# Down product of a SwiGLU layer: three stretches of eight contraction tiles by a seven-product scheme

## Chip, cores and metric

The kernel runs on one core of a Trainium2 chip. The metric is the device time of one execution in microseconds (us), median of several runs. Beside it stands one execution that was taken with the hardware profiler. Its engines are PE (matmul; PEld is its weight load), DVE (vector), ACT (scalar), POOL (GpSimd) and SP (which only issues DMAs here; a "q" behind an engine's name, as in SPq, is its queue).

## What is computed

One decoder layer on 544 tokens (512 of a prompt and 32 of samples), model width 2048. Its last part is the one that matters here:

```python
def layer_tail(x, attn_out, pool_out, w_out, norm_ffn, w_gate, w_up, w_down):
    x = x + jnp.concatenate([attn_out, pool_out], axis=-1) @ w_out
    h = rmsnorm(x, norm_ffn)
    return x + (jax.nn.silu(h @ w_gate) * (h @ w_up)) @ w_down
...
    y_prompt = rmsnorm(xp, norm_final)
    y_sample = rmsnorm(xs, norm_final)
```

All arrays are fp32. `w_gate` and `w_up` are 2048 x 5632, `w_down` is 5632 x 2048.

## The kernel before

Activations are kept transposed: features on 128 partitions, the 544 tokens along the free dimension. Width 2048 is 16 feature tiles, and the inner width 5632 is 44 tiles. Every factor of a product is split into a high and a low part (`whi`/`wlo` for weights, `H`/`L` for activations), and a product is three matmuls: high by high, high by low, low by high. The high part is a copy by ACT into a rounded type, the low part a subtraction on DVE. One matmul takes a 128 x 128 weight tile and 272 token columns, half of the 544.

**The gate and up products** (class `Winograd`, L874 to L993) use a scheme with seven block products in place of eight. Weights and activations are each cut into 2 x 2 blocks (output tiles p and p + 22 by the two halves of the contraction; the halves of the contraction by the two halves of the tokens). For each of 44 pairs of output tiles seven products P1 to P7 run on PE, each on sums or differences of blocks. Products are gathered in three PSUM tiles: X takes P1, then P6, P7 and P4 on top of it; Y takes P2; Z takes P5, then P3. After each step the partial sum is read before the next product is added to the same tile. The order within a pair is P2, P6, P5, P7, then P1 of the next pair, P4, P3. Sums of weight blocks are partly made by DMA: SP loads one block (`a11`, `a12`, `s1`, `s3`, `a22`), and POOL issues a second DMA that adds another block to `s1` and `s3`. DVE makes two more sums (`s2` at L949, `s4` at L961). `prep` and `high` (L920 to L965) run ACT and DVE up to four weight units ahead of PE.

In `ff_out` (L1003) ACT reads X after P1, P6 and P7 (`cp`, L1010), and DVE adds the pieces (L1013 to L1020). The results go to DRAM (`gd`).

**The down product** (L1233 to L1258) is plain. The 44 contraction tiles are taken in chunks of 12, 12, 12, 4 and 4. For each of the first four chunks, and for each of 16 output tiles `nt`, PE runs 6 matmuls for each contraction tile (`mm3`, L193: two halves of the tokens, three matmuls each). DVE then adds the PSUM tile to `x2` in SBUF, 544 columns at a time (L1252). Weights come through class `Stream` (L115): SP loads units of four contraction tiles into four `raw` buffers, ACT makes the high part (L143), DVE the low part (L148), some three units ahead of PE. The activations of the next chunk are loaded from `gd` by the generator `load_g` (L1155) one step for each `nt`; its first run starts in the last eight products of the gate and up part, with two steps for each product (L1195). The last four contraction tiles run in a loop of their own (L1268 to L1298) with 272 columns at a time, interleaved with the final norm and the output.

What sets the order: there is no scheduler. Each engine runs its instructions in the order in which the program was written, and waits at an instruction until what it needs is there. SP and POOL issue DMAs in order too, and each issue waits for a free buffer.

```python
            for u in range(n // UW):
                ...
                wh, wl, _ = ws2.next()
                gH, gL = groups[u]
                for i in range(UW):
                    k = UW * u + i
                    mm3(acc, wh, wl, gH, gL, i, i, k == 0, k == n - 1)
            ...
            nc.vector.tensor_add(two(x2[:, nt]), acc[:, :, :HALF], two(x2[:, nt]))
```

Of the kernel before, what the change touches and what calls it, by code (L numbers as in the profile page):

```python
# [18 lines left out]
P = 128  # L19
# [27 lines left out]
CHUNK = 12  # L47


F_ORDER = list(range(12)) + list(range(22, 34)) + list(range(12, 21)) + list(range(34, 37)) + [21] + list(range(37, 44))  # L50
# [113 lines left out]
def program(ctx, tc, a):  # L164
# [79 lines left out]
    UW = 4  # L244
# [15 lines left out]
    chunks = [(0, CHUNK), (CHUNK, CHUNK), (2 * CHUNK, CHUNK), (3 * CHUNK, UW), (3 * CHUNK + UW, UW)]  # L260
# [613 lines left out]
    class Winograd:  # L874


        P1, P2, P6, P5, P7, P4, P3 = range(7)
        ORDER = (P2, P6, P5, P7, P1, P4, P3)

        def __init__(self, pairs, raw, ops, sums, out):  # L880
            self.pairs, self.raw, self.ops, self.sums, self.out = pairs, raw, ops, sums, out

            seq = [(0, self.P1), (0, self.P2), (1, self.P1), (1, self.P2)]
            for i in range(len(pairs)):
                for p in self.ORDER:
                    seq.append((i + 1, p) if p == self.P1 else (i, p))
            self.seq = [x for n, x in enumerate(seq) if x[0] < len(pairs) and x not in seq[:n]]
            self.np = self.nh = self.nl = 0
            self.q, self.s, self.parts, self.bank, self.cp = {}, {}, {}, {}, {}
            self.later = deque()  # L890

        def load(self, upto):
            while self.nl < min(upto, len(self.pairs)):
                i = self.nl
                for what in ("a11", "a12", "s1", "s3", "a22"):
                    for u in range(2):
                        self.load_unit(i, what, u)
                self.nl += 1

        def load_unit(self, i, what, u):  # L900
            if (i, what, u) in self.q:
                return

            pool, tag, bufs = self.raw[{(0, "a12"): "a11", (1, "a11"): "a12"}.get((i, what), what)]
            t = pool.tile([P, UW, P], F32, name=what, tag=tag, bufs=bufs)
            w, n0, n1 = self.pairs[i]

            def part(r, c):
                k = (HK if c == 2 else 0) + UW * u
# [5 lines left out]
            if i:  # L915
                for x in terms[1:]:
                    nc.gpsimd.dma_start(t, part(*x), accum_op=ALU.add)
            self.q[i, what, u] = t

        def prep(self, upto):  # L920
            upto = min(upto, 2 * len(self.seq))
            while self.np < upto:
                while self.nh < min(2 * len(self.seq), self.np + 2) and self.ready(self.nh):
                    self.high()
                x, hi = self.parts[self.np]
                lo = wpa.tile([P, UW, P], F32R, tag="wlo", name="wlo", bufs=4)
                nc.vector.tensor_sub(lo, x, hi.bitcast(F32))  # L927
                self.parts[self.np] = (hi, lo)
                self.np += 1

        def ready(self, n):
            (i, p), u = self.seq[n // 2], n % 2
            needs = {self.P1: "a11", self.P2: "a12", self.P6: "a22"}
            return p not in needs or (i, needs[p], u) in self.q

        def high(self):
            if True:
                (i, p), u = self.seq[self.nh // 2], self.nh % 2
# [6 lines left out]
                elif p == self.P6:  # L945
                    x = self.s[i, u] = new("s2")
                    if i == 0:
                        nc.vector.tensor_add(r("s1"), r("s1"), r("a22"))
                    nc.vector.tensor_add(x, r("s1"), r("a11"))  # L949
                    if i == 0:  # L950
# [16 lines left out]
        def run(self, between=None):  # L967
            for n, (i, p) in enumerate(self.seq):
                if p == self.P1 and i != 1:
                    self.load(i + 2)  # L970
                if (i, p) == (0, self.P4):
# [6 lines left out]
                bh, bl = self.ops(p)  # L978
                for u in range(2):
                    self.prep(2 * n + u + 3)  # L980
                    ahead = self.nh - 1
                    if self.later and self.seq[ahead // 2][1] not in (self.P6, self.P7, self.P3):
                        self.later.popleft()()
                    wh, wl = self.parts.pop(2 * n + u)
                    for j in range(UW):
                        k = UW * u + j
                        first, last = start and k == 0, k == HK - 1
                        nc.tensor.matmul(o, wh[:, j], bh[:, k], start=first, stop=False, skip_group_check=True)  # L988
                        nc.tensor.matmul(o, wh[:, j], bl[:, k], start=False, stop=False, skip_group_check=True)  # L989
                        nc.tensor.matmul(o, wl[:, j], bh[:, k], start=False, stop=last, skip_group_check=True)  # L990
# [4 lines left out]
    fc = ExitStack()  # L995
    pC = None
    gd = [dr.tile([P, 2, TOK], F32, name=f"gd{i}") for i in range(HF)]
    pairs = [(a[w], p, p + HF) for p in range(HF) for w in ("w_gate", "w_up")]
# [48 lines left out]
    wn = Winograd(pairs, raws, lambda p: ops[p], None, ff_out)  # L1047
# [66 lines left out]
    pC = fc.enter_context(tc.tile_pool(name="pC", bufs=1, space=PSUM))  # L1114
# [16 lines left out]
    def between(n):  # L1131
# [11 lines left out]
        if 3 <= n < 7:  # L1143
            for k in (2 * n - 6, 2 * n - 5):
# [6 lines left out]
    ws2 = Stream(nc, wpa, [a["w_down"][nt][:, k:k + UW, :] for c, n in chunks[:-1] for nt in range(KT)  # L1151
                           for k in range(c, c + n, UW)], UW, 4, 2, 2)
    parts = {}

    def load_g(ci):  # L1155

        c0, n = chunks[ci]
        groups, staged = [], deque()
        parts[ci] = groups
# [7 lines left out]
        for f in range(n):  # L1167
            if f % UW == 0:
                b = 3 * (ci % 2) + f // UW
# [17 lines left out]
    g0 = load_g(0)  # L1187
    N1 = len(wn.seq)

    def between1(n):  # L1190
# [3 lines left out]
        if n >= N1 - 8:  # L1194
            run(g0, 2)  # L1195
# [6 lines left out]
    pac2 = ctx.enter_context(tc.tile_pool(name="pac2", bufs=1, space=PSUM))  # L1202
    x2 = fq.tile([P, KT, TOK], F32, name="x2")
    ssum3 = fq.tile([P, TOK], F32, name="ssum3")
    flip = [0]
# [7 lines left out]

    lastw, lastr = {}, {}

    def last_load(nt):
        if nt < KT:
            lastr[nt] = wpa.tile([P, UW, P], F32, tag="raw", name="raw", bufs=4)
            dma(lastr[nt], a["w_down"][nt][:, chunks[-1][0]:, :])

    def last_high(nt):
        if nt < KT:
            if nt % 4 == 0:
                b = (1, 2, 4, 5)[nt // 4]
                lastw[nt // 4] = [bp.tile([P, 17, P], F32R, name=f"w{x}{b}", tag=f"b{x}{b}") for x in "HL"]
            nc.scalar.activation(lastw[nt // 4][0][:, nt % 4 * UW:(nt % 4 + 1) * UW], lastr[nt], AF.Copy)

    def last_low(nt):
        if nt < KT:
            h, l = (x[:, nt % 4 * UW:(nt % 4 + 1) * UW] for x in lastw[nt // 4])  # L1230
            nc.vector.tensor_sub(l, lastr.pop(nt), h.bitcast(F32))

    for ci, (c0, n) in enumerate(chunks[:-1]):  # L1233
        groups = parts.pop(ci)
        ahead = load_g(ci + 1)
        for nt in range(KT):
            if ci == 0:
                dma(x2[:, nt], x1d[nt])
            acc = acc4()
            for u in range(n // UW):  # L1240
                if ci == nt == 0:
                    run(g0, 10 ** 6 if u == n // UW - 1 else 2)
                wh, wl, _ = ws2.next()
                gH, gL = groups[u]
                for i in range(UW):
                    k = UW * u + i
                    mm3(acc, wh, wl, gH, gL, i, i, k == 0, k == n - 1)
            if nt > 0:
                run(ahead, 1)
            if ci == 0 and wn.later:  # L1250
                wn.later.popleft()()
            nc.vector.tensor_add(two(x2[:, nt]), acc[:, :, :HALF], two(x2[:, nt]))  # L1252
            if ci == len(chunks) - 2 and nt >= KT - 3:
                last_load(nt - KT + 3)
                if nt == KT - 1:
                    last_high(0)
                    last_high(1)
                    last_low(0)  # L1258

    (gH, gL), = parts.pop(len(chunks) - 1)  # L1260
# [7 lines left out]
    for h in range(2):  # L1268
        c = slice(h * HALF, (h + 1) * HALF)
        for nt in range(KT):  # L1270
# [17 lines left out]
            else:  # L1288
                sq = fq.tile([P, HALF], F32, name="sq3", tag="sq3", bufs=2)
# [66 lines left out]
```

## Time and profile before

| | |
|---|---|
| time, median of 3 runs | 2271.59 us (2268.67 to 2272.65) |
| time of the profiled execution | 2271.41 us |
| its span, first to last instruction | 2269.6 us |
| PE busy | 2236.1 us, 99% of the span |
| PE weight load busy | 2142.4 us, 94% |
| DVE busy | 1276.4 us, 56% |
| ACT busy | 853.5 us, 38% |
| POOL busy | 154.5 us, 7% |
| mean granted TensorE clock | 0.995 |

A busy share is the mean over the whole span. In time order the stages are: the input projections and the attention up to about 572 us, the output projection up to 774 us, gate and up from 774 to 1717 us, the down product from 1718 us, its last four contraction tiles from 2203 us, and the end of the final norm with the output. What a change in one stage is worth is read in that stage. Rows overlap: PE rows are pipelined, and successive DVE and ACT rows start before the one in front has ended, so a row's duration is longer than the step from one row to the next.

### The profile page before, as it was taken

How to read it: one execution, taken by the hardware profiler on the slowest of the kernel's cores; microseconds unless marked ns; L12 is line 12 of the kernel's file. 1: busy time of each engine (PE TensorE's matmuls, PEld its weight loads, DVE VectorE, ACT ScalarE, POOL GpSimd, SP SyncE). 2: the span in 40 equal slices, each digit the busy share in tenths (PEclk: the TensorE clock that was granted, in tenths of full speed). 3: DMA queues.
4: the chain of work that ended last, by engine and by line, in shares of the span. 5: the costliest groups of instructions: out<-in, count | busy, mean ns of one | idle time of the engine just before them, and what ended most of it. 6: DMA issues, size and time to landing. Idle time of an engine off the chain costs nothing.

```text
span 2269.6 us, 44020 instructions
## 1 busy us (share of the span) xinstructions
PE 2236.1 (99%) x17540; PEld 2142.4 (94%) x17540; DVE 1276.4 (56%) x2487; ACT 853.5 (38%) x1621; POOL 154.5 (7%) x200
## 2 busy tenths in 40 slices
PE   8999999999999999999999999999999999999997
PEld 8878787879999999999999999999999999999997
DVE  7644445476544576666666666666675333333356
ACT  6322222223333454444444444444453222222235
POOL 0000000000000011111111111111110000000000
PEclk9999999999999999999999999999999999999998
DMA  5665656576544577777777777777765533333233
GB/s 192 203 221 202 224 200 234 204 206 157 139 126 136 171 193 180 192 196 176 193 197 174 190 201 173 190 202 174 191 171 162 162 119 114 123 103 90 84 109 111
DMA packets 196138, 384.93 MB, mean 170 GB/s; under 512 B 32907, under 2 KB 38171, under 8 KB 192348
## 3 DMA queue, kind: packets, MB, share of 16 engines
q1 hardware_dynamic: 170784, 336.84, 46.9%
q0 software_dynamic: 24768, 45.10, 11.9%
q8 instruction: 137, 2.24, 0.4%
q14 instruction: 69, 0.57, 0.1%
q10 hardware_dynamic: 380, 0.18, 0.0%
HBM read 352.47 MB, written 29.56 MB: 168 GB/s over the span
## 4 chain that ended last, share of the span: by engine, by line
PE 96%; DVE 2%; DMA 1%; ACT 1%; issue 1%; SPq 0%; DVEq 0%; ACTq 0%
PE acc L197 16%; PE acc L199 15%; PE acc L198 15%; PE X L989 8%; PE X L988 8%; PE X L990 8%; PE Z L989 4%; PE Z L988 4%; PE Z L990 4%; PE Y L989 2%; PE Y L990 2%; PE Y L988 2%; PE SO L635 1%; PE SS L588 1%; PE S L519 1%; PE O L565 1%
## 5 line engine op out<-in xcount | busy, mean ns | idle before, releaser
L989 PE MATMUL X<-bL,whi 128*128 128x272 f32 x1408 | 409.8, 291 | 0.1
L988 PE MATMUL X<-bH,whi 128*128 128x272 f32 x1408 | 406.8, 289 | 1.7 <-ACT cp L1010 1.7
L990 PE MATMUL X<-bH,wlo 128*128 128x272 f32 x1408 | 406.7, 289 | 0.0
L143 ACT ACTIVATE whi<-raw 128x512 fp32r<-128x512 f32 x352 | 217.8, 627 | 479.3 <-PE acc L198 441.5
L197 PE MATMUL acc<-gH,whi 128*128 128x272 f32 x1280 | 371.0, 290 | 0.6 <-DVE gu L1020 0.6
L199 PE MATMUL acc<-gH,wlo 128*128 128x272 f32 x1280 | 370.5, 289 | 0.0
L198 PE MATMUL acc<-gL,whi 128*128 128x272 f32 x1280 | 368.5, 288 | 0.0
L197 PE MATMUL acc<-hH,whi 128*128 128x272 f32 x992 | 304.6, 307 | 5.4 <-ACT whi L143 5.4
L199 PE MATMUL acc<-hH,wlo 128*128 128x272 f32 x992 | 287.9, 290 | 0.8 <-DVE wlo L148 0.8
L198 PE MATMUL acc<-hL,whi 128*128 128x272 f32 x992 | 286.0, 288 | 0.0
L148 DVE TENSOR_TENSOR wlo<-raw,whi 128x512 fp32r<-128x512 f32 x352 | 236.0, 684 | 86.4 <-issue 78.0
L963 ACT ACTIVATE whi<-s 128x512 fp32r<-128x512 f32 x352 | 212.1, 627 | 184.4 <-DVE s L949 118.4
L927 DVE TENSOR_TENSOR wlo<-s,whi 128x512 fp32r<-128x512 f32 x352 | 237.7, 685 | 59.5 <-ACT whi L963 59.5
L988 PEld LDWEIGHTS X<-bH,whi 128*128 128x128 f32 x1408 | 266.5, 189 | 1.9 <-ACT cp L1010 1.9
L990 PEld LDWEIGHTS X<-bH,wlo 128*128 128x128 f32 x1408 | 266.0, 189 | 0.0
L989 PEld LDWEIGHTS X<-bL,whi 128*128 128x128 f32 x1408 | 265.2, 188 | 0.3 <-DVE bL L1100 0.3
L197 PEld LDWEIGHTS acc<-hH,whi 128*128 128x128 f32 x992 | 187.2, 189 | 63.5 <-issue 55.4
L197 PEld LDWEIGHTS acc<-gH,whi 128*128 128x128 f32 x1280 | 240.9, 188 | 0.8 <-issue 0.8
L198 PEld LDWEIGHTS acc<-gL,whi 128*128 128x128 f32 x1280 | 241.3, 189 | 0.0
L199 PEld LDWEIGHTS acc<-gH,wlo 128*128 128x128 f32 x1280 | 240.8, 188 | 0.2 <-DVE wlo L148 0.2
L927 DVE TENSOR_TENSOR wlo<-a,whi 128x512 fp32r<-128x512 f32 x264 | 181.0, 685 | 66.1 <-ACT whi L963 49.1
L1252 DVE TENSOR_TENSOR x<-acc,x 128x544 f32<-128x544 f32 x64 | 46.4, 724 | 258.9 <-PE acc L199 258.9
(223 smaller groups left out, 4503.1 us busy)
## 6 DMA issues: line engine op xcount, KB each, us to landing
raw<-w_down SPq DMA_DIRECT2D x176, 256.0 KB, 2.7
a<-w_gate SPq DMA_DIRECT2D x132, 256.0 KB, 4.2
a<-w_up SPq DMA_DIRECT2D x132, 256.0 KB, 6.0
raw<-w_in SPq DMA_DIRECT2D x128, 256.0 KB, 3.6
kv<-cv SPq DMA_DIRECT2D x28, 1024.0 KB, 6.4
s<-w_gate SPq DMA_DIRECT2D x88, 256.0 KB, 5.2
s<-w_up SPq DMA_DIRECT2D x88, 256.0 KB, 5.2
s<-w_up POOLq DMA_DIRECT2D x88, 256.0 KB, 5.5
```

The source lines that it names most:

```text
L143: nc.scalar.activation(hi[:, :n], t[:, :n], AF.Copy)
L148: nc.vector.tensor_sub(lo[:, :n], t[:, :n], hi[:, :n].bitcast(F32))
L197: nc.tensor.matmul(o, wh[:, i, :], xh[:, kt, c], start=start, stop=False)
L198: nc.tensor.matmul(o, wh[:, i, :], xl[:, kt, c], start=False, stop=False)
L199: nc.tensor.matmul(o, wl[:, i, :], xh[:, kt, c], start=False, stop=stop)
L519: nc.tensor.matmul(ps[s][:, :w], q[r, c], x[r, :w], start=(k == 0), stop=(k == 2))
L927: nc.vector.tensor_sub(lo, x, hi.bitcast(F32))
L963: nc.scalar.activation(hi, x, AF.Copy)
L988: nc.tensor.matmul(o, wh[:, j], bh[:, k], start=first, stop=False, skip_group_check=True)
L989: nc.tensor.matmul(o, wh[:, j], bl[:, k], start=False, stop=False, skip_group_check=True)
L990: nc.tensor.matmul(o, wl[:, j], bh[:, k], start=False, stop=last, skip_group_check=True)
L1252: nc.vector.tensor_add(two(x2[:, nt]), acc[:, :, :HALF], two(x2[:, nt]))
```

## The change

The 44 contraction tiles of the down product are now taken in parts of 8, 8, 4, 8, 4, 8 and 4. The second, fourth and sixth (8 tiles each) run by the seven-product scheme, with output tiles i and i + 8 as a pair (8 pairs) and each product over 4 contraction tiles (`n_units` 1: one weight unit, 12 matmuls, where gate and up have two units and 24 matmuls). The others run as before, with two PSUM tiles in place of four (`acc_tile` for `acc4`). Each of the seven partial sums is added to or taken from `x2` in SBUF straight from PSUM by DVE (`down_out`); there is no ACT read of X. The block operands of four contraction tiles are made by `load_pairs` while the plain part ahead of the stretch runs; the activations for the plain part behind it by `load_g` while the stretch runs. Weight blocks `a12`, `s1`, `s3` and `a22` have three buffers of one unit each, `a11` the four `raw` buffers. The first run of `load_g` has one step for each product in place of two. The class takes these as arguments, and leaves out the start that gate and up have (`cold`).

```diff
-CHUNK = 12
+PARTS = ((False, 0, 8), (True, 8, 8), (False, 16, 4), (True, 20, 8), (False, 28, 4), (True, 32, 8), (False, 40, 4))
+F_ORDER = [22 * h + c // 2 + i for _, c, n in PARTS for h in range(2) for i in range(n // 2)]
...
-            seq = [(0, self.P1), (0, self.P2), (1, self.P1), (1, self.P2)]
+            seq = [(0, self.P1), (0, self.P2), (1, self.P1), (1, self.P2)] if cold else [(0, self.P1)]
...
-                for u in range(2):
-                    self.prep(2 * n + u + 3)
+                for u in range(self.nu):
+                    self.prep(self.nu * n + u + 3)
...
-            run(g0, 2)
+            run(g0, 1)
...
+    raws2 = {"a11": (wpa, "raw", 4)}
+    for w in ("a12", "s1", "s3", "a22"):
+        raws2[w] = (fq, w, 3)
+
+    def down_out(wn, i, p, o):
+        q = lambda x, y: x2[:, i + x * HK, y * HALF:(y + 1) * HALF]
+        if p in (wn.P1, wn.P2):
+            nc.vector.tensor_add(q(0, 0), o, q(0, 0))
+        elif p in (wn.P6, wn.P3):
+            nc.vector.tensor_add(q(0, 1), o, q(0, 1))
+        elif p in (wn.P5, wn.P7):
+            nc.vector.tensor_sub(q(1, 1), q(1, 1), o)
+        else:
+            nc.vector.tensor_sub(q(1, 0), q(1, 0), o)
...
+    def load_pairs(c0, out):
...
+            high(0)
+            sub(0, b11, 1.0, b12)
+            sub(1, b22, -1.0, t[:, 0])
+            yield
+            high(1)
+            sub(2, b22, 1.0, b12)
+            sub(3, b21, -1.0, t[:, 1])
+            yield
+            high(2)
+            low(0)
+            low(1)
+            yield
+            low(2)
+            yield
...
+    def plain(n, groups, ws, steps, ahead):
+        for nt in range(KT):
...
+            acc = acc_tile()
...
+            nc.vector.tensor_add(two(x2[:, nt]), acc[:, :, :HALF], two(x2[:, nt]))
+
+    groups, ws = first_groups, ws2
+    for ci in range(1, len(PARTS) - 1, 2):
+        c0 = PARTS[ci][1]
+        slots = []
+        wp = Winograd([(a["w_down"], i, i + HK, c0, c0 + UW) for i in range(HK)], 1, raws2,
+                      lambda p, k, s=slots: [x[:, PLACE[p]] for x in s[k]], fq, down_out, False)
+        plain(PARTS[ci - 1][2], groups, ws, load_pairs(c0, slots), wp)
...
+        def between2(n, g=g, ws=ws, left=NS_):
+            left -= n + 1
+            if 4 <= n and n % 4 == 0:
+                run(g, 1)
...
+        wp.run(between2)
```

How this moves instructions is shown at three places. First, DVE inside a plain stretch of the down product, before, one output tile with its three weight units (L148 makes a low part, L1252 adds a finished PSUM tile to `x2`):

```order
L1252 TENSOR_TENSOR x2_21108<-acc2_22661,x2_21108 128x544
L148 TENSOR_TENSOR wlo_22756<-raw_22633,whi_22722 128x512
L148 TENSOR_TENSOR wlo_22786<-raw_22666,whi_22754 128x512
L148 TENSOR_TENSOR wlo_22816<-raw_22696,whi_22784 128x512
L1252 TENSOR_TENSOR x2_21108<-acc_22753,x2_21108 128x544
```

And DVE inside the first seven-product stretch of the change, from P6 of one pair to P1 of the next but one (L929 makes a low part, L963 the sum `s4`, L951 the sum `s2`, L1260 to L1266 take one product's sum from X, Y or Z into `x2`):

```order
L1262 TENSOR_TENSOR x2_21081<-X_22293,x2_21081 128x272
L929 TENSOR_TENSOR wlo_22387<-a11_22281,whi_22367 128x512
L1264 TENSOR_TENSOR x2_21081<-x2_21081,Z_22384 128x272
L963 TENSOR_TENSOR s4_22402<-a12_22176,s2_22311 128x512
L929 TENSOR_TENSOR wlo_22406<-a22_22184,whi_22385 128x512
L1264 TENSOR_TENSOR x2_21081<-x2_21081,X_22293 128x272
L929 TENSOR_TENSOR wlo_22436<-s4_22402,whi_22404 128x512
L1260 TENSOR_TENSOR x2_21081<-X_22433,x2_21081 128x272
L951 TENSOR_TENSOR s2_22454<-s1_22285,a11_22281 128x512
L929 TENSOR_TENSOR wlo_22458<-a12_22283,whi_22434 128x512
L1266 TENSOR_TENSOR x2_21081<-x2_21081,X_22293 128x272
```

There is now one read of PSUM for each weight unit, and two of seven reads stand behind a sum as well as a low part.

Second, DVE at the end of that stretch, products P6, P5, P7, P4 and P3 of the last pair (L148 with `raw` belongs to the plain part that follows):

```order
L1262 TENSOR_TENSOR x2_21081<-X_23123,x2_21081 128x272
L963 TENSOR_TENSOR s4_23213<-a12_22987,s2_23141 128x512
L929 TENSOR_TENSOR wlo_23217<-a22_22995,whi_23195 128x512
L1264 TENSOR_TENSOR x2_21081<-x2_21081,Z_23212 128x272
L929 TENSOR_TENSOR wlo_23240<-s4_23213,whi_23215 128x512
L1264 TENSOR_TENSOR x2_21081<-x2_21081,X_23123 128x272
L148 TENSOR_TENSOR wlo_23271<-raw_23231,whi_23267 128x512
L1266 TENSOR_TENSOR x2_21081<-x2_21081,X_23123 128x272
L1262 TENSOR_TENSOR x2_21081<-Z_23212,x2_21081 128x272
```

Here no P1 of a next pair stands between P7 and P4, and the first low part of the next plain part stands ahead of the last two reads.

Third, ACT at the end of the gate and up part, before (L1163 makes the high part of a down activation in `load_g`, L1010 reads X after P7, L1018 after P4):

```order
L963 ACTIVATE whi<-s_20990 128x512
L1163 ACTIVATE gH_20964<-gst 128x544 x2
L1010 ACTIVATE cp<-X 128x272
L963 ACTIVATE whi<-s_21019 128x512
L1163 ACTIVATE gH_20964<-gst 128x544 x2
L1018 ACTIVATE gu<-X 128x272
```

and in the change, the same place (line numbers are those of the changed kernel):

```order
L965 ACTIVATE whi<-s_20968 128x512
L1164 ACTIVATE gH_20791<-gst 128x544
L1013 ACTIVATE cp<-X 128x272
L965 ACTIVATE whi<-s_20993 128x512
L1164 ACTIVATE gH_20946<-gst 128x544
L1021 ACTIVATE gu<-X 128x272
```

One copy of a down activation stands ahead of each read of X, where there were two.

## Rows read from the trace of the kernel before

**Rows 1.** The page: span, and busy time, share and instructions of each engine.

```profile
span 2269.6 us, 44020 instructions
PE 2236.1 (99%) x17540; PEld 2142.4 (94%) x17540; DVE 1276.4 (56%) x2487; ACT 853.5 (38%) x1621; POOL 154.5 (7%) x200
```

**Rows 2.** Windows: stretch, length, busy PE PEld DVE ACT POOL (instructions), clock, DMA, GB/s.

```profile
1000.00:1600.00 600.00, 600.00 (x4765) 600.00 (x4764) 408.73 (x683) 280.95 (x526) 99.62 (x114) 1.00 0.74 188
1719.00:2202.00 483.00, 483.00 (x3832) 483.00 (x3832) 167.64 (x257) 118.42 (x191) 0.00 (x0) 1.00 0.38 117
```

**Rows 3.** Waits of PE, 1600 to 2270 us: for whom, us in total, times, longest.

```profile
PE X L988 <- ACT cp L1010: 1.7, 1, 1.7
...
PE acc L1281 <- DVE wL L1231: 1.2, 1, 1.2
PE acc L197 <- DVE gu L1020: 0.6, 1, 0.6
```

**Rows 4.** Groups by shape, 1690 to 2270 us: count | busy, mean ns | idle before.

```profile
L148 DVE TENSOR_TENSOR wlo<-raw,whi 128x512 fp32r<-128x512 f32 x160 | 105.6, 686 | 57.1 <-issue 54.8 <-ACT whi L143 2.3
L1252 DVE TENSOR_TENSOR x<-acc,x 128x544 f32<-128x544 f32 x64 | 46.4, 724 | 258.9 <-PE acc L199 258.9
L1164 DVE TENSOR_TENSOR gL<-gst,gH 128x544 fp32r<-128x544 f32 x44 | 31.2, 718 | 0.5 <-ACT gH L1163 0.4
L1283 DVE TENSOR_TENSOR x<-acc,x 128x272 f32<-128x272 f32 x32 | 14.1, 441 | 10.3 <-PE acc L1281 8.2
L1285 DVE TENSOR_TENSOR ssum<-ssum,sq 128x272 f32<-128x272 f32 x29 | 12.5, 431 | 0.0
```

**Rows 5.** Groups by shape, 900 to 1650 us (gate and up).

```profile
L927 DVE TENSOR_TENSOR wlo<-s,whi 128x512 fp32r<-128x512 f32 x283 | 191.2, 685 | 50.3 <-ACT whi L963 50.3
L917 POOL DMA_DIRECT2D s<-w_gate x68 | 59.7, 921 | 317.2 <-DVE wlo L927 189.8 <-DMA s<-w_gate 88.5 <-DVE gu L1020 17.8
```

**Rows 6.** Timeline of DVE in gate and up: start, duration, line, operation, [idle before].

```profile
1201.71 0.44 DVE L1015 SCALAR_TENSOR_TENSOR gu<-Z,cp 128x272 f32<-128x272 f32 x1 [2.70 <-ACT cp L1010]
1202.07 0.68 DVE L927 TENSOR_TENSOR wlo<-a,whi 128x512 fp32r<-128x512 f32 x1
1202.66 0.68 DVE L961 TENSOR_TENSOR s<-a,s 128x512 f32<-128x512 f32 x1
1203.27 0.68 DVE L927 TENSOR_TENSOR wlo<-a,whi 128x512 fp32r<-128x512 f32 x1
```

**Rows 7.** Timeline in gate and up: a product's last matmul, and ACT's read of X.

```profile
1203.98 0.29 PE L990 MATMUL X<-bH,wlo 128*128 128x272 f32 x1
...
1204.31 0.40 ACT L1010 ACTIVATE cp<-X 128x272 f32<-128x272 f32 x1 [0.23 <-PE X L990]
```

**Rows 8.** Timelines of ACT and PE at the end of gate and up.

```profile
1708.85 0.63 ACT L963 ACTIVATE whi<-s 128x512 fp32r<-128x512 f32 x1 [1.58 <-DVE s L961]
1709.39 1.19 ACT L1163 ACTIVATE gH<-gst 128x544 fp32r<-128x544 f32 x2
1710.48 0.37 ACT L1010 ACTIVATE cp<-X 128x272 f32<-128x272 f32 x1
...
1710.91 0.39 PE L988 MATMUL X<-bH,whi 128*128 128x272 f32 x1 [1.67 <-ACT cp L1010]
```

**Rows 9.** DMA issues, 900 to 1650 us: count, KB each, median us to landing.

```profile
s<-w_gate SPq DMA_DIRECT2D x69, 256.0 KB, 5.2
s<-w_gate POOLq DMA_DIRECT2D x68, 256.0 KB, 6.5
```

**Rows 10.** Waits of SP's queue, 900 to 1650 us.

```profile
SPq L914 <- DVE s L961: 311.0, 72, 12.8
```

**Rows 11.** Matmuls of L197: count, ns min/median/max, first and last start.

```profile
L197 PE MATMUL acc<-hH,whi x992: 282/289/594, 5.4 to 571.8; 128*128 128x272 f32 x199
```

**Rows 12.** Windows at the end of the program, columns as in rows 2.

```profile
2250.00:2260.00 10.00, 7.07 (x51) 6.68 (x49) 5.96 (x18) 4.38 (x10) 0.00 (x0) 0.91 0.28 102
2260.00:2270.00 10.00, 0.00 (x0) 0.00 (x0) 5.02 (x8) 0.00 (x0) 0.00 (x0) 0.50 0.65 223
```

More of the change, by code (lines that the diff above doesn't have):

```diff
@@ L995, in program @@
     fc = ExitStack()
+    pcx = ExitStack()
     pC = None
     gd = [dr.tile([P, 2, TOK], F32, name=f"gd{i}") for i in range(HF)]
[L998 removed]
+    pairs = [(a[w], p, p + HF, 0, HK) for p in range(HF) for w in ("w_gate", "w_up")]
     raws = {"a11": (wpa, "raw", 4)}
@@ L1148, in between, with stream, load_g @@
                                                op1=ALU.subtract)
[L1151 to L1159, printed above, removed]
+    def stream(c0, n):
+        return Stream(nc, wpa, [a["w_down"][nt][:, k:k + UW, :] for nt in range(KT) for k in range(c0, c0 + n, UW)],
+                      UW, 4, 2, 2)
+    def load_g(c0, n, tags, groups):
+        staged = deque()
         def split():
@@ new lines, in last_low @@
+    def last_low(nt):
+        if nt < KT:
+            h, l = (x[:, nt % 4 * UW:(nt % 4 + 1) * UW] for x in lastw[nt // 4])
+            nc.vector.tensor_sub(l, lastr.pop(nt), h.bitcast(F32))
+    def plain(n, groups, ws, steps, ahead):
+        for nt in range(KT):
+            if ws is ws2:
+                dma(x2[:, nt], x1d[nt])
+            acc = acc_tile()
+            for u in range(n // UW):
+                if ws is ws2 and nt == 0:
+                    run(g0, 10 ** 6 if u == n // UW - 1 else 2)
+                wh, wl, _ = ws.next()
+                if nt == KT - 1 and u == n // UW - 1:
+                    ahead.prep(2)
+                gH, gL = groups[u]
+                for i in range(UW):
+                    k = UW * u + i
+                    mm3(acc, wh, wl, gH, gL, i, i, k == 0, k == n - 1)
+            if nt >= KT - 2:
+                ahead.load(nt - KT + 3)
+            if wn.later:
+                for _ in range(min(2, len(wn.later))):
+                    wn.later.popleft()()
+            else:
+                run(steps, 10 ** 6 if nt == KT - 1 else 2 if ws is ws2 or nt == 0 else 1)
+            nc.vector.tensor_add(two(x2[:, nt]), acc[:, :, :HALF], two(x2[:, nt]))
@@ new lines, in program @@
+    groups, ws = first_groups, ws2
[5 more added lines that the diff above has]
+        plain(PARTS[ci - 1][2], groups, ws, load_pairs(c0, slots), wp)
+        _, c1, n1 = PARTS[ci + 1]
+        groups, end = [], ci == len(PARTS) - 2
+        g = load_g(c1, n1, ((ci // 2) % 2,), groups)
+        ws = None if end else stream(c1, n1)
+        NS_ = len(wp.seq)
+        def between2(n, g=g, ws=ws, left=NS_):
+            left -= n + 1
+            if 4 <= n and n % 4 == 0:
+                run(g, 1)
+            if end:
+                if 1 <= left <= 3:
+                    last_load(3 - left)
+                if left < 2:
+                    last_high(1 - left)
+            elif left == 3:
+                ws.load(4)
+            elif left == 1:
+                ws.prep(1)
+        wp.run(between2)
+        run(g)
+        if end:
+            last_low(0)
+        else:
+            ws.prep(2)
@@ L1211, in acc4 @@
         return acc_tile()
[L1214 to L1260, printed above, removed]
+    (gH, gL), = groups
     todo, squares = deque(), deque()
```

99 lines of the change are left out of this document (69 added, 30 removed).

## Prediction

> **What bounds the kernel now.** I read the page's busy times first [rows 1]: PE is busy for 99% of the span, DVE for 56%, ACT for 38%. A mean over the span hides stages, so the windows came next. In 600 us of the gate and up part and in 483 us of the down product PE is never idle, and the granted clock is 1.00, the upper of its two levels [rows 2]. From these rows comes the unit of everything below: 483.00 us over 3832 matmuls is 0.1260 us for each in the plain down product, and 600.00 over 4765 is 0.1259 in the seven-product scheme of gate and up. A PE row lasts longer than that because rows overlap; the step between matmuls is what counts. The third view is who PE waited for from 1600 us on [rows 3]: three waits bear on the change, 1.7, 1.2 and 0.6 us, all where one stage meets the next. So the down product is bound by the number of matmuls, and DVE and ACT have room in it: DVE is busy for 168 of 483 us there, and for 409 of 600 us in gate and up [rows 2].
>
> **What the change removes.** A plain stretch of 8 contraction tiles has 16 output tiles x 8 x 6 = 768 matmuls. The seven-product stretch has 8 pairs x 7 products x 4 tiles x 3 = 672. Three stretches save 3 x 96 = 288 matmuls; at 0.1260 us that is **36.3 us**. The plain parts and the last four tiles keep theirs. This saving is whole only if PE stays as gapless as it was, so the rest of the working asks where it could wait.
>
> **Does DVE keep up inside a stretch?** A product now takes 12 x 0.126 = 1.51 us and a pair 7 x 1.51 = 10.6 us; a stretch of 8 pairs 84.7 us. By the order, DVE does for each pair seven low parts, two sums and seven reads of PSUM into x2. The lengths of its rows are 0.685 us for a low part [rows 4, 5], 0.68 for a sum [rows 6], and 0.441 for an add of 272 columns out of PSUM into x2 [rows 4], which is the very operation that the change adds. Rows overlap, though: in the timeline a low part or sum starts 0.60 us after the one in front, and the low part behind a 272-column read of PSUM starts 0.36 us after it [rows 6]. By these steps a pair takes 7 x 0.60 + 2 x 0.60 + 7 x 0.36 = 7.9 us of DVE; by whole durations, which is the other bound, 4.8 + 1.4 + 3.1 = 9.3 us. The four low parts of load_g add 4 x 0.72 = 2.9 us to a stretch [rows 4], 0.4 us a pair. Both bounds, 8.3 and 9.7, lie below 10.6. I take the first, since back-to-back rows are what DVE will have.
>
> **Does DVE read in time?** PE may not add P7 to X before DVE has read X after P6, nor P4 before the read after P7. One other product lies between in each case, 1.51 us. A read starts some 0.04 us after the last matmul's row ends [rows 7] and lasts 0.44, so about 1.0 us is spare. Against it stands what is queued ahead of the read. In the piece of DVE's order shown first, the read after P7 has a sum and a low part between it and the read before: 0.36 + 0.60 + 0.60 = 1.56 us against 1.51, so it is 0.05 us late. A low part of load_g may come on top, 0.72 at most [rows 4]: 0.8 in all, still inside 1.0. Low parts are made two products ahead, so a lag of that size does not reach them. Cost inside a stretch: nothing, and what covers it is that 1.0 us.
>
> **At the end of a stretch** the cover is gone. The last pair has no next P1, so P4 follows P7 directly (second place of the order) and waits for the read: 0.04 + 0.44, say 0.5 us with the signal, three times: **+1.6 us**. Bounds: 0.4 a time if nothing is ahead, 1.7 a time as in the one such wait of the trace, where ACT read X behind two other copies [rows 8].
>
> **At the end of gate and up** that same wait shrinks. There ACT copied two down activations (1.19 us) ahead of its read of X after P7, and PE stood for 1.67 us [rows 8]; P7 had ended at 1709.24. The change leaves one copy ahead of the read, and fewer low parts on DVE ahead of the sum that ACT waited for. With ACT free by 1709.3, the read costs its own 0.4 us plus 0.05: **-1.2 us**. Bounds: 0 (nothing gained) and -1.2. The 0.6 us of waiting that follows, where the plain part starts, I leave as it is: its first low part still stands behind the last read of Z.
>
> **At the other borders** of stretches I count nothing. Into a plain part, the first low part stands ahead of the last two reads. Into a stretch, the operands of load_pairs are finished during the plain part: for each output tile DVE has a low part (0.69), an add (0.72) and at most one subtraction of 1088 columns, which I put at 1.3 us from the rows of 272 and 544 columns (0.431 and 0.72) [rows 4]; that is 2.7 us in the 24 x 0.126 = 3.02 us that a plain tile of four takes. Two accumulators in place of four suffice for the same reason. At the last border, the low part that PE waited for by 1.2 us [rows 3] now stands behind a read of 272 columns instead of 544, 0.44 for 0.72 [rows 4]: **-0.3 us**.
>
> **The weights.** A pair needs five loads by SP and two accumulating ones by POOL, 256 KB each, in 10.6 us; gate and up needs twice that in twice the time, with the 16 DMA engines busy 0.74 of it [rows 2]. The longest chain is that of s1: load 5.2 us, issue on POOL 0.9, accumulation 6.5 [rows 5, 9], then some 3 us until its last reader is done, 15.6 us for one buffer. Three buffers turn this into one pair in 5.2 us, half of what is asked. Cost: nothing.
>
> **The sum**, against the profiled execution's own 2271.4 us (0.2 below the median): 2271.4 - 36.3 + 1.6 - 1.2 - 0.3 = 2235.2, so **2235 us**. With the bounds of the terms, and PE's step between 0.1259 and 0.1260, its own range is 2231 to 2241. Throughout, 0.2% of the time, 4.5 us, is about what can be told from no change: faster means below 2267.0, slower above 2276.1.
>
> **Rivals.**
>
> *DVE's reads come late.* DVE serves two more things per product than before, and a lag over 1.0 us stops PE at P7 and P4. For it: by whole durations the read after P7 comes 0.44 + 0.68 + 0.69 = 1.81 us after the one before, 0.3 late, and with a low part of load_g 1.0, exactly the limit. Against it: 0.60 steps are in the trace, and DVE has slack in the other products. If PE stood 0.3 us at both handovers of all 24 pairs, 48 x 0.3 = 14 us come back: about 2250.
>
> *The accumulating loads come late, and the change is slower.* The place is the sum s2, which waits for s1 in DVE's queue; behind it stand a low part and the next read of X, so PE stops too. It decides when a pair takes over 10.6 + 1.5 = 12.1 us, for then the seven-product stretch is longer than the 768 plain matmuls. That would be so if the three buffers were used one after another, as a queue that issues in order can bring about: SP stood 311 us behind the sum s4 for a free buffer in 750 us of gate and up [rows 10]. One pair would then take the chain's 15.6 us, 24 x 5.0 = 120 us more: 2355. Against it: in those 750 us PE lost nothing. The Trainium skill (GPSIMD Engine Reference, "8. Key points") speaks for this rival: GpSimd shares its SBUF interfaces with VectorE and contends with vector instructions that have two SBUF inputs, which is what low parts and sums are. The trace does not bear it out where it can be seen: a low part lasts 0.685 us beside POOL's issues and 0.686 without any [rows 4, 5], and PE lost nothing.
>
> *The clock falls.* PE stops briefly at many handovers and is granted the lower level. In the trace the granted clock falls only where PE has run dry: 0.91 in the last slice with matmuls, 0.50 behind them [rows 12]. A matmul's row lasts 289 ns as a rule and 594 ns at the longest [rows 11]; taking that as the lower level, a stretch run wholly at it costs 85 us more. One seventh of the three stretches would eat the saving; a tenth gives 2261. The Trainium skill (TensorE: Matmul & The Clock Gate, "A second HAM failure mode: psum-queue depth-cycling") describes a kernel that lost throughput so, with small pauses between groups on changing banks. Gate and up changes banks in just this way at 1.00, so the trace does not agree here.
>
> *The change does not do what it says.* Shorter products could run at a longer step per matmul, so that fewer matmuls take the same time. Against it: groups of 24 (gate and up) and of 72 (plain) have the same step to 0.1%. It would give about 2271.
>
> **How the numbers follow.** The forecast 0.76, since both kinds of stretch already run without a gap and the new operations fit with room. Late reads 0.14, late loads 0.05, the clock 0.03 (of it 0.02 slower), no effect 0.02. Faster: 0.76 + 0.14 + 0.01 = 0.91. Same 0.02. Slower 0.05 + 0.02 = 0.07. The range goes from the forecast's lower end to just beyond the late reads at 0.3 us: 2231 to 2252, which leaves out the last three cases and the worse half of the late reads, 0.17 or so.
>
> **What would show it.** Right: 288 fewer matmuls at 0.126 us; PE gapless in the three stretches but for three waits of about 0.5 us of P4 for DVE's read of X; DVE busy for 75 to 90% of a stretch; clock 1.00. Wrong: PE waits at P7 or P4 in every pair, charged to the reads of X; DVE idle at s2, waiting for an accumulating DMA; a clock below 1.00 in a stretch; or matmuls a longer step apart.

## The result and the profile after

The changed kernel takes 2243.74 us (median of 4 runs, 2243.03 to 2247.45), the kernel before 2271.64 on the same chip (2268.67 to 2272.65). The ratio is 0.9883, with a 95% interval of 0.9865 to 0.990. The forecast was 2235 us: the direction is as forecast and the range holds the time, but the profiled execution (2244.42 us) is 9.2 us over the sum, above the forecast's own range. The range held the time only because it reached up to 2252 for late reads, which did not come; that the loss found below fell inside it is luck. Those 9 us are what the rest looks for.

The head of the page of the kernel after answers to [rows 1]:

```profile
span 2242.7 us, 44120 instructions
PE 2201.8 (98%) x17252; PEld 2106.1 (94%) x17252; DVE 1429.3 (64%) x2819; ACT 899.0 (40%) x1705; POOL 196.4 (9%) x248
```

PE has 17252 matmuls for 17540, the 288 fewer of the prediction. By the starts of the first matmul of each stage, the time went so:

| stage | before | after | difference |
|---|---|---|---|
| up to gate and up | 774.6 | 776.5 | +1.9 |
| gate and up | 943.2 | 939.2 | -4.0 |
| down product, to its last four tiles | 484.6 | 460.7 | -23.9 |
| last four tiles, to the end of the span | 67.1 | 66.3 | -0.8 |

The first stage has the same code in both. Over the profiles of this study it ended between 773.8 and 777.0 us, so up to 3 us of a difference between two single executions mean nothing. Of the -4.0, 1.2 was forecast, 0.8 is a wait that moved into the down product, and about 2 come at the start of gate and up, which the change does not touch: from 776 to 800 us the clock was 0.86 before and 1.00 after. The row that matters is the third: the forecast's terms for it, -36.3 and +1.6, make -34.7, and it was -23.9.

Windows of the kernel after, columns as in [rows 2]: 82 us inside the second seven-product stretch, then 12 us behind the end of the first stretch and 4 us behind the end of the second.

```profile
1948.00:2030.00 82.00, 82.00 (x652) 82.00 (x651) 66.74 (x126) 33.08 (x58) 11.35 (x13) 1.00 0.66 166
...
1904.00:1908.00 4.00, 1.61 (x13) 1.39 (x12) 0.93 (x3) 1.50 (x3) 0.00 (x0) 1.00 0.90 315
1908.00:1912.00 4.00, 3.26 (x18) 3.29 (x19) 4.00 (x8) 2.25 (x4) 0.00 (x0) 0.71 0.26 73
1912.00:1916.00 4.00, 4.00 (x29) 4.00 (x29) 2.56 (x4) 0.95 (x2) 0.00 (x0) 0.86 0.26 70
...
2048.00:2052.00 4.00, 4.00 (x34) 4.00 (x33) 4.00 (x8) 2.59 (x4) 0.00 (x0) 1.00 0.44 124
```

Inside the stretch everything is as forecast: PE has no gap, 82.00 us over 652 matmuls is 0.1258 us each, DVE is busy for 66.74 of 82 us (81%), the clock is 1.00. The loss lies at the borders. PE's waits from 1600 to 2250 us (for whom, us in total, times, longest):

```profile
PE acc L197 <- ACT whi L143: 3.1, 1, 3.1
PE acc L197 <- DVE x L1312: 3.0, 1, 3.0
...
PE X L990 <- ACT whi L143: 1.2, 2, 0.6
PE acc L199 <- DVE wlo L148: 0.9, 1, 0.9
PE acc L1377 <- DVE x L1262: 0.6, 1, 0.6
PE X L990 <- DVE x L1264: 0.6, 1, 0.6
PE X L990 <- ACT cp L1013: 0.5, 1, 0.5
```

The first two were not forecast. They stand in the two plain parts of four tiles, behind the second output tile, when PE needs the accumulator of the first for the third. PE's timeline at the first of them, and at one of the three short waits of P4 for X:

```profile
1895.38 0.29 PE L992 MATMUL X<-oH,wlo 128*128 128x272 f32 x1
1896.29 0.37 PE L990 MATMUL X<-oH,whi 128*128 128x272 f32 x1 [0.62 <-ACT whi L143]
1896.49 0.29 PE L991 MATMUL X<-oL,whi 128*128 128x272 f32 x1
...
1905.32 0.29 PE L199 MATMUL acc<-gH,wlo 128*128 128x272 f32 x1
1908.74 0.36 PE L197 MATMUL acc<-gH,whi 128*128 128x272 f32 x1 [3.13 <-ACT whi L143]
1908.94 0.28 PE L198 MATMUL acc<-gL,whi 128*128 128x272 f32 x1
```

These rows also price a stop. The short one shows 0.62 us of idleness, but from 1895.38 to 1896.49 two matmul steps took 1.11 us in place of 0.25, so it costs 0.86: the idle time counts only from the end of a 0.29 us row, not from the 0.126 us step, and the first step after the stop is longer. By the same reckoning the long stop costs 3.62 - 0.25 = 3.37 us, and its fellow at 2047.55 us (3.00 of idleness) 3.24. After the first, the clock is 0.71 and 0.86 for 4 us each, which is 4 x 0.29 + 4 x 0.14 = 1.7 us more. Together 8.3 us, in this one execution.

What holds PE up there is seen in the queues, first SP's timeline with its waits, then the timelines of DVE and ACT (start, duration, line, operation, [idle before]):

```profile
1887.73 14.92 SPq L129 DMA_DIRECT2D raw<-w_down  x4
1902.70 1.85 SPq L1200 DMA_DIRECT2D gst<-gd  x4
```

What SP's weight loads wait for from 1860 to 1915 us (us in total, times, longest); both are operations that free a `raw` buffer:

```profile
SPq L129 <- DVE s L951: 21.2, 3, 10.3
SPq L129 <- DVE wlo L148: 15.6, 4, 8.7
```

```profile
1899.96 1.28 DVE L148 TENSOR_TENSOR wlo<-raw,whi 128x512 fp32r<-128x512 f32 x2
1905.83 0.44 DVE L1211 SCALAR_TENSOR_TENSOR to<-gst 128x272 f32<-128x272 f32 x1 [4.59 <-DMA gst<-gd]
1907.52 0.44 DVE L1211 SCALAR_TENSOR_TENSOR to<-gst,to 128x272 f32<-128x272 f32 x1 [1.24 <-DMA gst<-gd]
1907.87 0.72 DVE L1312 TENSOR_TENSOR x<-acc,x 128x544 f32<-128x544 f32 x1
```

```profile
1905.89 0.43 ACT L1214 ACTIVATE oH<-gst 128x272 fp32r<-128x272 f32 x1 [7.31 <-DMA gst<-gd]
1906.23 0.61 ACT L143 ACTIVATE whi<-raw 128x512 fp32r<-128x512 f32 x1
```

The loads of `load_pairs` (`gst`, L1200) for the next stretch are written behind four weight loads, and those four, which wait for a free buffer, take 14.92 us to issue. So the `gst` loads go out only at 1902.70. DVE's first subtraction on them waits 4.59 us and the second 1.24. Behind these in DVE's order stands the add (L1312) that empties the first of two accumulators; it runs at 1907.87, some 5 us after PE has finished that tile: in the experiment delay below, where nothing stands ahead of it, the same add runs at 1902.22. ACT likewise stands 7.31 us at its copy of `gst` with the next high part (L143) behind it.

### The profile page after: what moved, and what is told of

It is laid out like the page before. It is cut to its first block, busy times and chain, and to the rows that moved or that the text cites. A ratio compares the mean times of both kernels' runs of the same rounds, so it can differ in the third digit from the quotient of the medians.

```text
span 2242.7 us, 44120 instructions
## 1 busy us (share of the span) xinstructions
PE 2201.8 (98%) x17252; PEld 2106.1 (94%) x17252; DVE 1429.3 (64%) x2819; ACT 899.0 (40%) x1705; POOL 196.4 (9%) x248
## 3 DMA queue, kind: packets, MB, share of 16 engines
q0 software_dynamic: 31680, 57.69, 15.6%
## 4 chain that ended last, share of the span: by engine, by line
PE 94%; DMA 2%; DVE 2%; issue 1%; ACT 1%; SPq 0%; DVEq 0%; ACTq 0%
PE acc L197 12%; PE acc L199 11%; PE acc L198 11%; PE X L991 10%; PE X L990 10%; PE X L992 10%; PE Z L991 5%; PE Z L990 5%; PE Z L992 5%; PE Y L991 2%; PE Y L990 2%; PE Y L992 2%; PE SO L634 1%; PE SS L587 1%; PE S L518 1%; PE O L564 1%
## 5 line engine op out<-in xcount | busy, mean ns | idle before, releaser
L929 DVE TENSOR_TENSOR wlo<-s,whi 128x512 fp32r<-128x512 f32 x448 | 303.4, 685 | 59.7 <-ACT whi L965 59.7
L197 PE MATMUL acc<-hH,whi 128*128 128x272 f32 x992 | 304.5, 307 | 6.2 <-ACT whi L143 6.2
L199 PE MATMUL acc<-hH,wlo 128*128 128x272 f32 x992 | 287.7, 290 | 0.8 <-DVE wlo L148 0.8
L929 DVE TENSOR_TENSOR wlo<-a,whi 128x512 fp32r<-128x512 f32 x336 | 230.3, 686 | 66.5 <-ACT whi L965 49.6
L197 PEld LDWEIGHTS acc<-hH,whi 128*128 128x128 f32 x992 | 187.2, 189 | 64.4 <-issue 55.3
L143 ACT ACTIVATE whi<-raw 128x512 fp32r<-128x512 f32 x256 | 156.6, 623 | 204.6 <-PE acc L198 163.5
L965 ACT ACTIVATE whi<-a 128x512 fp32r<-128x512 f32 x336 | 207.3, 624 | 48.1 <-DVE wlo L929 20.1
L148 DVE TENSOR_TENSOR wlo<-raw,whi 128x512 fp32r<-128x512 f32 x256 | 172.7, 683 | 28.9 <-issue 23.2
L199 PEld LDWEIGHTS acc<-hH,wlo 128*128 128x128 f32 x992 | 187.1, 189 | 1.5 <-DVE wlo L148 1.5
L198 PEld LDWEIGHTS acc<-hL,whi 128*128 128x128 f32 x992 | 187.7, 189 | 0.1
L197 PE MATMUL acc<-gH,whi 128*128 128x272 f32 x512 | 149.0, 291 | 6.1 <-ACT whi L143 3.1
L199 PE MATMUL acc<-gH,wlo 128*128 128x272 f32 x512 | 148.9, 291 | 0.9 <-DVE wlo L148 0.9
L199 PE MATMUL acc<-mH,wlo 128*128 128x272 f32 x512 | 148.8, 291 | 0.1
L197 PE MATMUL acc<-mH,whi 128*128 128x272 f32 x512 | 148.9, 291 | 0.0
```

The costliest lines, as they stand in the source:

```text
L143: nc.scalar.activation(hi[:, :n], t[:, :n], AF.Copy)
L148: nc.vector.tensor_sub(lo[:, :n], t[:, :n], hi[:, :n].bitcast(F32))
L197: nc.tensor.matmul(o, wh[:, i, :], xh[:, kt, c], start=start, stop=False)
L198: nc.tensor.matmul(o, wh[:, i, :], xl[:, kt, c], start=False, stop=False)
L199: nc.tensor.matmul(o, wl[:, i, :], xh[:, kt, c], start=False, stop=stop)
L965: nc.scalar.activation(hi, x, AF.Copy)
```

## The experiments

Four theories were put to the test. **A**: the long waits come because DVE and ACT stop, in order, at work on `gst` that isn't there yet. Its rival **R**: the weights themselves are late at that place, whatever `load_pairs` does. **H**: the three short X waits come from the order P7, P4 of a stretch's last pair, that is, from DVE's read, though the list of waits names ACT's high part for two of them. And for DVE inside a stretch, the step between rows against the whole duration of rows.

**prefetch: the loads of `load_pairs` go out during the stretch in front.**

```diff
+    slots = []
+    steps = load_pairs(PARTS[1][1], slots)
     for ci in range(1, len(PARTS) - 1, 2):
...
-        plain(PARTS[ci - 1][2], groups, ws, load_pairs(c0, slots), wp)
+        plain(PARTS[ci - 1][2], groups, ws, steps, wp)
+        slots = []
+        steps = None if ci == len(PARTS) - 2 else load_pairs(PARTS[ci + 2][1], slots)
...
+            if left == 20 and steps:
+                run(steps, 1)
```

> Theory A: the two 3 us waits of PE at the start of the second and third plain parts come from the loads of the down activations for load_pairs. SP issues them behind weight loads that wait for a raw buffer, and DVE and ACT stand at the operations on them, ahead of the add that frees the accumulator and of the next high part. Here the first of these loads is issued 20 products before the end of the stretch ahead. By A both waits go (3.13 + 3.00 us, and 0.16 each for the row's tail that the idle time leaves out), and with the first the 8 us of lower clock behind it (4 us at 0.71, 4 at 0.86: 1.7 us): 2243.7 - 8.2 = 2235.5. Rival R: the weights themselves are late (the profile names ACT's high part of a weight for the first wait); nothing about them changes here, so the waits stay and the time is 2243.7.

Measured: 2237.3 us (2234.72 to 2240.96), ratio to before 0.9847 (0.9832 to 0.9861); the kernel before, measured beside it, took 2272.34. The down product takes 452.6 us for 460.7, 8.1 less. SP's timeline and DVE's at the same border:

```profile
1854.01 0.89 SPq L1200 DMA_DIRECT2D gst<-gd  x2
```

```profile
1901.27 0.43 DVE L1211 SCALAR_TENSOR_TENSOR to<-gst,to 128x272 f32<-128x272 f32 x1
1901.62 0.72 DVE L1312 TENSOR_TENSOR x<-acc,x 128x544 f32<-128x544 f32 x1
```

The loads are out 49 us earlier, DVE does not stop for them, and the add runs at 1901.62. Both long waits are gone, and so is the lower clock: 1900 to 1946 us has 46.00 us of PE at 1.00.

**delay: the first loads stay where they are, the work on them comes two output tiles later.** (The loads for the second pair of blocks move with that work.)

```diff
-                run(steps, 10 ** 6 if nt == KT - 1 else 2 if ws is ws2 or nt == 0 else 1)
+                run(steps, 10 ** 6 if nt == KT - 1 else 2 if ws is ws2 else {0: 1, 1: 0, 2: 2, 3: 2}.get(nt, 1))
```

> The loads stay where they are, but in the second and third plain parts the first operations on them are moved from output tile 0 to tile 2. By A nothing then stands behind a late load, although it is as late as before: DVE no longer waits some 5 us for it ahead of an add, both PE waits go, about 2235.5. By R the weights are as late as before: 2243.7. If A is right but the loads are later still than tile 2, part of the wait comes back, 2236 to 2240.

Measured: 2236.32 us (2235.21 to 2237.63), ratio 0.9843 (0.9827 to 0.986); down product 452.6 us. SP, then DVE:

```profile
1887.32 13.87 SPq L129 DMA_DIRECT2D raw<-w_down  x4
1901.24 1.75 SPq L1200 DMA_DIRECT2D gst<-gd  x2
```

```profile
1902.22 0.72 DVE L1312 TENSOR_TENSOR x<-acc,x 128x544 f32<-128x544 f32 x1 [1.38 <-PE acc L199]
...
1906.48 0.43 DVE L1211 SCALAR_TENSOR_TENSOR to<-gst 128x272 f32<-128x272 f32 x1
```

The weight loads and the first `gst` loads are about as late as in the change itself (1901.24 for 1902.70), yet PE waits for neither: the add now stands ahead of the subtraction and runs as soon as PE has finished the tile. So the weights weren't late, and R falls. The change's own rows agree: the low parts for all three tiles were done by 1901.24, over 7 us before PE went on. A is shown from two sides: bring the loads forward, or take what must not wait out from behind them.

**lastpair: the last pair of a stretch runs P3 ahead of P4.**

```diff
+            if not cold:
+                self.seq[-2:] = self.seq[:-3:-1]
```

> In the last pair of each stretch P3 is put between P7 and P4. Theory H: the three waits of 0.62 us at P4 are for DVE's read of X after P7, and go: 3 x (0.62 + 0.16) = 2.3 us less, 2241.4, and no wait of PE at X in the down product. Rival: two of the three are put down to ACT's high part of the next plain part's weights; if that is their cause they stay, and the time is 2243.7.

Measured: 2241.53 us (2240.82 to 2243.88), ratio 0.9866 (0.9851 to 0.9881). No wait for X is left in the down product. So H holds. The high part (L143) that the list of waits names for two of the three is one of the next plain part, which P4 does not use; the third was charged to DVE's read, rightly. The long waits remain, 2.59 and 2.43 us here, in one row of the waits:

```profile
PE acc L197 <- DVE x L1314: 5.0, 2, 2.6
```

**best: both, prefetch and lastpair.**

> Early loads and the new order of the last pair together: by A and H 2243.7 - 8.2 - 2.3 = 2233.2, and PE without a wait from the start of the second plain part to the last four contraction tiles. If either theory falls, its share is missing: 2235.5 or 2241.4.

Measured: 2234.14 us (2233.01 to 2235.93), ratio 0.9832 (0.9818 to 0.9847): faster than both kernels, 38.2 us under the kernel before that was measured beside it, with an interval that does not meet that of the change (0.9865 to 0.990). Its waits of PE from 1700 us, without those of the final norm and of the end of gate and up:

```profile
...
PE acc L199 <- DVE wlo L148: 0.9, 1, 0.9
PE acc L1384 <- DVE x L1268: 0.6, 1, 0.6
...
```

None is left inside the down product but the one at its start (L199) and the one at its last border (L1384). The down product takes 449.9 us, 2.6 less than with prefetch alone: 3 x 0.86, the price of a short stop read above.

**dve_half and dve_full: one more DVE sum of 512 columns behind every second product of a stretch, or behind every one.** The sum goes to a tile that is overwritten before anything reads it.

```diff
+            if n % 2 == 0:
+                nc.vector.tensor_add(ssum3[:, :512], x2[:, 0, :512], x2[:, 1, :512])
```

(`n % 1` in dve_full.)

> One more 128x512 addition on DVE at every other product of the stretches (28 or 29 a stretch; its result is not used). If DVE's cost is the step between rows, a pair takes 7.9 + 0.4 + 3.5 x 0.60 = 10.4 us of DVE against PE's 10.6: PE stands now and then at the reads of X, but little comes on top, 2244 to 2250. If it is the rows' whole duration, 9.3 + 0.4 + 3.5 x 0.68 = 12.1 us: 24 x 1.5 = 36 us more, 2280.

> The same addition at every product. By steps 7.9 + 0.4 + 7 x 0.60 = 12.5 us a pair, DVE is the bound: 24 x 1.9 = 46 us more, 2290. By durations 9.3 + 0.4 + 7 x 0.68 = 14.5 us: 24 x 3.9 = 94 us more, 2337.

Measured: 2246.23 us (2245.77 to 2246.69) and 2297.92 us (2296.3 to 2299.55), with 2273.25 for the kernel before. A window of dve_half's first stretch, and the first two rows of dve_full's waits of PE:

```profile
1816.00:1898.00 82.00, 81.17 (x639) 80.56 (x638) 79.87 (x155) 33.52 (x58) 10.48 (x12) 1.00 0.60 145
```

```profile
PE X L990 <- DVE x L1262: 20.8, 23, 1.7
PE X L990 <- DVE x L1264: 16.9, 24, 2.0
```

In dve_half DVE is busy for 79.87 of 82 us and PE still loses little: 639 matmuls in this window, where the change has 645 in the same 82 us, 0.8 us less work. Whole durations would have made 2280. In dve_full DVE is over the limit, and the rival of the late reads appears just where the prediction put it, at P7 in 23 and at P4 in all 24 pairs. The cost over the change is 54 us; by steps 46 were expected, by durations 94. Steps are the right measure; the other 8 us I did not trace.

**bufs2 and bufs1: two buffers, or one, for the blocks `a12`, `s1`, `s3` and `a22`.**

```diff
-        raws2[w] = (fq, w, 3)
+        raws2[w] = (fq, w, 2)
```

(1 in bufs1.)

> Two buffers in place of three for a12, s1, s3 and a22. If the chain of s1 (15.6 us for one buffer) sets what buffers are worth, two give a pair in 7.8 us, less than PE's 10.6: no change, 2243.7. If the queue that issues in order makes the buffers work one after another, up to 24 x 5.0 = 120 us more, 2364.

> One buffer each: a pair takes the chain's 15.6 us in place of 10.6, 24 x 5.0 = 120 us more, 2364, with DVE and ACT waiting for the accumulating DMAs. If PE still keeps its 10.6 us, the chain is far shorter than I put it.

Measured: 2242.8 us (2241.79 to 2243.81), no change; and 2394.82 us (2393.74 to 2395.9), 151 over the change, where 120 were expected. In bufs1, DVE's costliest wait and PE's from 1815 to 2300 us, and windows in its first two stretches:

```profile
DVE s L951 <- DMA s<-w_down: 130.4, 20, 7.8
```

```profile
PE Y L992 <- DVE wlo L929: 101.2, 20, 6.3
```

```profile
1820.00:1940.00 120.00, 84.08 (x566) 82.53 (x564) 57.52 (x110) 28.71 (x49) 12.16 (x14) 0.85 0.49 122
1990.00:2120.00 130.00, 100.31 (x709) 98.97 (x708) 70.38 (x132) 33.52 (x57) 12.76 (x15) 0.91 0.46 114
```

This is the prediction's slower rival at work: DVE stands at the sum `s2` for the accumulating load, and PE behind DVE. A pair takes 10.6 + 151 / 24 = 16.9 us, where the chain alone was put at 15.6. The clock of 0.85 and 0.91 is part of that, and I did not separate the two. With two buffers nothing of it is left, so three are not at the edge.

**gstep2: the first run of `load_g` in two steps a product again.**

```diff
-            run(g0, 1)
+            run(g0, 2)
```

> The first run of load_g has two steps for each of the last eight products of gate and up again, as before the change. If the shorter wait at the end of gate and up (0.49 us in place of 1.67) comes from having one copy in place of two ahead of ACT's read of X, PE's wait there goes back to 1.2 to 1.7 us and the time is 1 us longer, within what the runs scatter. If it comes from something else, the wait stays at 0.49.

Measured: 2243.86 us (2243.46 to 2244.27), 0.9876 (0.9848 to 0.9905): no change. PE waits 0.58 us at the end of gate and up, not the 1.67 of [rows 8]. The edit did not bring back what it was to bring back: the first part has 8 tiles now, and with two steps a product their copies are all done before the read, so that ACT comes to it from a high part alone:

```profile
1710.98 0.63 ACT L965 ACTIVATE whi<-s 128x512 fp32r<-128x512 f32 x1 [1.58 <-DVE s L963]
1711.52 0.38 ACT L1013 ACTIVATE cp<-X 128x272 f32<-128x272 f32 x1
```

ACT waits 1.58 us for the sum ahead of its high part, just as in [rows 8], but the two copies that stood there between the high part and the read of X are missing, and PE's wait is 1.09 us shorter, the time by which those copies moved the read. So copies ahead of the read made the wait of before. The one step in place of two is not needed for the shorter wait: with the shorter first part, two steps leave no copy there either.

The run also shows the two long waits again, in a down product with the same code as the change:

```profile
PE acc L197 <- DVE x L1312: 2.3, 1, 2.3
...
PE acc L197 <- ACT whi L143: 2.2, 1, 2.2
```

Here they are shorter, the clock behind both is 1.00, and the down product takes 457.5 us, 4.9 over that of prefetch. So the 8.1 us of the change's profiled execution is the upper end of what these waits cost in the executions seen here.

## Why the prediction came out as it did, step by step

DVE's timeline inside a stretch, from one read of PSUM to the next, for the second point below:

```profile
1841.18 0.44 DVE L1264 TENSOR_TENSOR x<-x,Z 128x272 f32<-128x272 f32 x1 [0.38 <-PE Z L992]
1841.54 0.68 DVE L963 TENSOR_TENSOR s<-a,s 128x512 f32<-128x512 f32 x1
1842.14 0.68 DVE L929 TENSOR_TENSOR wlo<-a,whi 128x512 fp32r<-128x512 f32 x1
1842.74 0.43 DVE L1264 TENSOR_TENSOR x<-x,X 128x272 f32<-128x272 f32 x1
```

- **288 fewer matmuls, -36.3: right.** 0.1258 us each in a stretch. The version without the long and the short waits (best) is 38.2 us under before; the terms -36.3, -1.2 and -0.3 make -37.8, though the last did not come (see below).
- **DVE keeps up and reads in time, 0: right**, by steps, as chosen. From read to read it is 0.36 + 0.60 + 0.60 = 1.56 us, to the hundredth what was worked out; the second read does not wait for PE, and PE does not wait for it.
- **P4 behind P7 at the end of a stretch, +1.6: mechanism right, size off.** Three waits of 0.62 us cost 0.86 each, 2.6 in all. I had left out what the row of a matmul hides and the restart.
- **End of gate and up, -1.2: right.** PE waits 0.49 us for 1.67. The forecast had ACT free by about the time at which P7 ends; in the change ACT is done earlier and stands idle for 1.27 us until the read (below). That copies ahead of the read were the cause, gstep2 shows by an order without any.

```profile
1707.25 0.64 ACT L1164 ACTIVATE gH<-gst 128x544 fp32r<-128x544 f32 x1
1709.17 0.40 ACT L1013 ACTIVATE cp<-X 128x272 f32<-128x272 f32 x1 [1.27 <-PE X L992]
```

- **The other borders, 0: this step failed.** It read: "At the other borders of stretches I count nothing", because "the operands of load_pairs are finished during the plain part". They are finished in time; that was the wrong question. I added up how long DVE needs for them in a plain tile (2.7 of 3.02 us) and took for granted that their input is there. SP issues in order, and the loads stood behind four weight loads that themselves waited for buffers; and I did not ask what is queued behind the waiting instruction, which is the add that empties one of only two accumulators, and the next high part on ACT. Measured: 8.1 us between the down products of prefetch and the change, by the rows 3.37 + 3.24 + 1.7; 4.9 us with the shorter waits of gstep2; and 6.4 and 7.4 us from the change's median to those of prefetch and delay. That two accumulators suffice belongs to this step: two cover one late tile of 3.02 us, and the add was over 5 us late. Whether four would have covered it, no run tried. The first stretch was spared: nothing of this is in the plain part of 8 tiles ahead of it.
- **The start of the down product, 0, and the last border, -0.3.** PE now waits 0.88 us at the third matmul (L199) where it had waited 0.62 at the first, some 0.3 us more. At the last border 0.63 us ahead of the last four tiles take the place of the 1.2 behind it [rows 3], but those tiles and the end took only 0.8 us less, which the stop ahead of them eats up.
- **Weights, 0: right**, and bufs2 shows that even two buffers suffice.
- **The sum.** 2235.2 + 8.1 + 1.0 (X waits) + 0.3 + 0.3 = 2244.9, against 2244.42 in the profiled execution. The remaining 0.5 is less than the first stage alone varies.
- **The rivals.** Late reads and late loads did not come; dve_full and bufs1 show that both mechanisms are real, and how far off they were. For the late loads a page had spoken: the Trainium skill (GPSIMD Engine Reference, "8. Key points") says that GpSimd contends with vector instructions of two SBUF inputs. The trace does not agree here either: low parts in the down product after, beside POOL's 44 issues, have a mean of 0.682 us, against 0.686 without any [rows 4]. But POOL does nothing there except issue DMAs; other work of POOL was not run. The falling clock came as a small piece, 1.7 us behind one long stop, and not in the stretches. The prediction's reading that the clock falls only at the end of the program missed a place: in the kernel before it is 0.66 from 790 to 800 us, behind a wait of PE of 2.99 us. (Its 85 us for a stretch at the lower level would be 89 by the 594 and 289 ns that it names; nothing hangs on it.)

## What to carry to other kernels

When work is moved in among other work, follow its input back to the DMA queue: ask behind which loads its load is issued and what buffers those wait for, not only whether the engine has time. Then look at what stands behind the first instruction that touches that input on each in-order engine; with two accumulators, an add that waits for somebody else's data stops PE within one further tile. Either issue such loads a stage early or let the work on them come a tile or two later; each removed both long waits here, 5 to 8 us.

## What the runs showed of the hardware that I had not expected

**The clock behind a stop of 2.0 to 3.1 us fell in some cases and not in others.** In the change it fell to 0.71 and 0.86 behind the stop of 3.13 us, and stayed at 1.00 behind that of 3.00. In lastpair, windows at its first long wait (2.59 us):

```profile
1904.00:1908.00 4.00, 1.41 (x12) 1.22 (x10) 1.73 (x4) 2.00 (x4) 0.00 (x0) 0.92 0.77 264
1908.00:1912.00 4.00, 4.00 (x22) 4.00 (x23) 3.32 (x7) 1.65 (x3) 0.00 (x0) 0.66 0.37 88
```

There it fell to 0.66, a mean between the two levels, and behind the stop of 2.43 us it stayed at 1.00. Seven of the profiled executions (the change, lastpair, the two dve runs, the two bufs runs and gstep2) have these two long stops. Behind six of the 14 the clock fell, behind eight it stayed at 1.00, and stops of 2.03 us did both: it fell in dve_full and stayed in dve_half. So the length of the stop alone does not tell it; what does stays open. The Trainium skill (TensorE: Matmul & The Clock Gate, "A second HAM failure mode: psum-queue depth-cycling") tells of a kernel that lost throughput by frequent small pauses between groups of matmuls; the stretches here change banks without a pause, so this does not bear on them. bufs1, with 20 waits of up to 6.3 us, ran at 0.85 and 0.91, which agrees with it, though its pauses are not small.

**A stop of PE costs more than its idle time shows**: 0.86 us for 0.62 of idleness, 3.37 for 3.13.
